# A conformer and dilated attention block on one core: attention issued in its written order, fillers split half a weight at a time, conv norm with eight diagonals

## The chip, the cores and the metric

The kernel runs on one core of a Trainium2 chip. The metric is the time of one execution on the device in microseconds: 1806.95 us, the median of three runs (1806.19 to 1810.14). The core's engines have a queue of instructions each: TensorE (PE, with its weight loads shown apart as PEld), VectorE (DVE), ScalarE (ACT), GpSimd (POOL) and SyncE (SP, which issues nearly all transfers here). An engine issues its queue in order, and a wait at the head of a queue holds all that is behind it.

## What is computed

One block over 1024 tokens of width 1024, in float32:

```
h = rms_norm(x); z = h @ w_in              # glu halves, q, k, v, two gates
a = a_val * sigmoid(a_gate)
a = silu(rms_norm(causal_depthwise_conv(a, 31 taps))); y_a = a @ w_conv_out
q, k = rms_norm per head (16 heads of 64)
o = mix of three dilated window attentions with alibi slopes; y_b = o @ w_attn_out
x = x + (sigmoid(g_a) * y_a + sigmoid(g_b) * y_b) @ w_out
h = rms_norm(x); u = depthwise_conv(h @ w_up, 3 taps)
x = x + (silu(u_gate) * u_val) @ w_down
```

The three windows share one softmax: the mask tensor of a head holds the slope's term and the logarithm of how many windows contain a pair, so the kernel takes one softmax over all causal keys.

## The kernel before, in words

Products are float32 in three passes of float32r: each operand is split into a high part (ScalarE, L76) and a low part (VectorE, L77), and high by high, high by low and low by high are summed in PSUM (`gemm_half`, L103 to L111, yields after each group of three products; such a group is called a step here). `stage` loads 512 KB of a weight into one of four `raw` buffers, `wsplit` splits it whole into one of four `whi` and `wlo` pairs.

Stages in order: the first norm and its transposes; the glu products; q, k and v, beside which VectorE computes the 31-tap convolution of eight channel blocks (`conv_branch`, `cacc`); the conv norm; attention; the output product of attention with the merge of the gates (`yb`, from L596 on); the output product, the second norm, and the feed-forward part.

Two products have nothing to wait for but their inputs and are used as fillers: the sixteen gate blocks (`gate_steps`) and, once the conv branch has been written to `da`, its output product `ya` (`side_work`). They make 384 steps. Of these, `COVER` gives three portions ahead of attention (24, 16 and 52), and `FILL` with `credit` doles out the rest in attention; what is left runs at the end of it.

The conv norm (L434 to L454): column sums of squares as products into `pss`, a reciprocal root on GpSimd (`crs`), which is spread over columns by eight products of `ones` with a diagonal tile `dg` (two buffers), copied to `sqacc`; then eight scalings by VectorE, eight SiLUs by ScalarE and eight stores to `da`.

Attention works in steps of half a head (four query blocks of 128). `step(cur, prev)` interleaves the scores of the current half with the flips and weightings of the half before. `score` (L502): two products per 512 keys into `s` (two buffers of two PSUM banks), the row minimum of negated, masked scores on VectorE (L513), the exponential with its sum on ScalarE (L515), the reciprocal on VectorE (L516), the scaling of the row on GpSimd (L517). `flip` (L520): up to four transposes of 128 x 128 into a PSUM bank `pp`, then the split into `ph` (ScalarE) and `pl` (VectorE). `weigh` (L531): two products with v into the bank `o`, up to two flips later. At the step's end ScalarE copies half of `o` to `ot` (L575) and VectorE adds it to the other half (L576). The banks `pp`, `o`, `gate` and `ya` share four buffers.

The order of instructions on each engine comes from a scheduler that runs a timing model over the program at build time and prefers what is written earlier among what it holds ready. Inside `tc.manual_schedule(engines=...)` the named engines take the order in which the instructions are written. Before the change, this holds in the first norm and at one place behind attention (L781), not in attention. A tile waits for the release of the buffer that it takes; a pool opened with `reuse_waits="tile"` waits for the tiles that lay there before.

Of the kernel before, what the change touches and what calls it, by code (L numbers as in the profile page):

```python
# [12 lines left out]
F32 = mybir.dt.float32  # L13
# [7 lines left out]
P = 128  # L21
# [13 lines left out]
FILL = (5.5, 9.5)  # L35
COVER = (24, 16, 52)
# [14 lines left out]
def block_kernel(ctx: ExitStack, tc: tile.TileContext, x, g1, g2, pack, mask,  # L51
# [95 lines left out]
    def gate_steps(hT):  # L147
        def gate(c, w, half):
            gp = bank_ps(f"gate_{c}_{half}")
            yield from gemm_half(gp, w, hT, half)  # L150
            sg = cst.tile([P, 512], F32, tag="f2", bufs=2, name=f"gs_{c}_{half}")
            act.activation(sg, gp, AF.Identity, bias=pk[:, C_GB + c : C_GB + c + 1])
            sp.dma_start(dgate[c][:, half * 512 : half * 512 + 512], sg)

        for c in range(12):
            w = wpiece(w_ch[16 + c], f"gt{c}")
            for half in range(2):
                yield from gate(c, w, half)
        ws = [wpiece(w_ch[16 + c], f"gt{c}") for c in range(12, 16)]
        for half in range(2):  # L160
            for c in range(12, 16):
                yield from gate(c, ws[c - 12], half)
            if half == 0:
                yield "half"
# [20 lines left out]
    with tc.tile_pool(name="ph1", bufs=1) as p1:  # L185
        t4 = lambda name, dt=F32: p1.tile([P, 1024], dt, tag="t4", bufs=4, name=name)
        g1r = p1.tile([1, D], F32, tag="csq", bufs=1, name="g1r")
# [168 lines left out]
        def conv_branch():  # L356
            accs = []
            for c in range(8):
# [13 lines left out]
                else:  # L372
                    sq = p1.tile([P, T], F32, tag="csq", bufs=1, name=f"csq_{c}")
# [5 lines left out]
        def qkv_head(ch, tt, ps):  # L379
# [7 lines left out]
            sq = p1.tile([P, 512], F32, tag="sq", bufs=2, name=f"sq_{ch}_{tt}")  # L387
# [5 lines left out]
            qn = p1.tile([P, 512], F32, tag="qn", bufs=3, name=f"qn_{ch}_{tt}")  # L393
# [4 lines left out]
        def qkv_tail(ch, tt, qn):  # L398
# [4 lines left out]
            qh = p1.tile([P, 512], F32R, tag="qh", bufs=2, name=f"qh_{ch}_{tt}")  # L403
            ql = p1.tile([P, 512], F32R, tag="ql", bufs=2, name=f"ql_{ch}_{tt}")
# [23 lines left out]
        gates = gate_steps(hT)  # L428
        for _ in range(COVER[0]):
            next(gates)  # L430
# [9 lines left out]
        for _ in range(COVER[1]):  # L440
            next(gates)
# [13 lines left out]
        for _ in range(COVER[2]):  # L455
            next(gates)


    with tc.tile_pool(name="ph2", bufs=1, reuse_waits="tile") as p2:
        def side_work():  # L460

            left = []
            for t in gates:
                if t == "half":
                    aT = hb_tiles(hb1, "aT")
                    left = list(range(0, KT, 2))
                    wait = 0
                elif left:
                    if wait == 0:
                        load_split(aT, da, 0, "a", [left.pop(0)])  # L470
                    wait = (wait + 1) % 7
                yield
            assert not left
            left = list(range(0, KT, 2))
            for c0 in (0, 4):
                ws = [wpiece(w_co[c], f"co{c}") for c in range(c0, c0 + 4)]
                for half in range(2):
                    for c in range(c0, c0 + 4):
                        if left:
                            load_split(aT, da, 1, "a", [left.pop(0)])  # L480
                        yp = bank_ps(f"ya_{c}_{half}")
                        yield from gemm_half(yp, ws[c - c0], aT, half)
# [64 lines left out]
        def step(cur, prev):  # L547
# [45 lines left out]
        for _ in filler:  # L593
            pass
# [537 lines left out]
```

## Time and profile before

| what | value |
|---|---|
| median of three runs | 1806.95 us |
| the profiled execution | 1806.91 us |
| its span | 1805.1 us |
| mean granted TensorE clock | 0.994 |
| TensorE busy | 1768.3 us, 98% |
| VectorE, ScalarE busy | 1314.1 us, 769.8 us |
| first product of a gate | 470.2 us |
| first score of attention | 540.0 us |
| last weighting of attention | 940.9 us |
| first product of `yb` | 969.2 us |

The times in the lower half are starts in the profiled execution. A product of 512 columns is shown as 0.389 us long, but products overlap: where TensorE is dense, it issues some 222 in 50 us, one in 0.225 us. How dense a stretch is can be told from the number of products as well as from the busy time. The granted clock (PEclk) shows where TensorE runs at half speed for a while though it is busy.

### The profile page before, as it was taken

The numbers are of one execution on the slowest core, as the hardware profiler recorded it, in microseconds if no ns is written. First come the engines' busy times: TensorE is split into PE (matmuls) and PEld (weight loads), VectorE is DVE, ScalarE is ACT, GpSimd is POOL, SyncE is SP. The second block draws the span as 40 slices with busy tenths as digits, with TensorE's granted clock in tenths as the row PEclk, the third lists the DMA queues.
The fourth block names the chain that finished last, engine by engine and source line by source line (L and its number), as shares of the span: only waits on it lengthen the run. The fifth ranks groups of instructions, "written<-read, shape, count | busy, mean of one in ns | idle before, by whom it ended". The sixth has DMA issues, their size and how long they took to land.

```text
span 1805.1 us, 22538 instructions
## 1 busy us (share of the span) xinstructions
PE 1768.3 (98%) x8248; PEld 1461.6 (81%) x8248; DVE 1314.1 (73%) x1805; ACT 769.8 (43%) x1203; POOL 182.5 (10%) x193
## 2 busy tenths in 40 slices
PE   8999999999999999999999999899999999999999
PEld 6888888888888888878888877778888888878887
DVE  7999999999635666665654563587777677679863
ACT  5111132223246666665654342455454454543431
POOL 1000142132003222122210000000000000000000
PEclk9999999999999999999999999999999999999999
DMA  5111145345468536674527566532222222399851
GB/s 215 47 47 47 43 133 175 105 135 169 136 222 231 153 122 184 196 206 148 149 76 260 178 231 213 192 105 86 89 71 93 82 80 84 117 328 327 288 175 47
DMA packets 145809, 270.16 MB, mean 150 GB/s; under 512 B 11681, under 2 KB 60961, under 8 KB 145698
## 3 DMA queue, kind: packets, MB, share of 16 engines
q1 hardware_dynamic: 145696, 268.72, 46.2%
q8 instruction: 65, 1.06, 0.3%
q14 instruction: 46, 0.38, 0.1%
q10 hardware_dynamic: 2, 0.00, 0.0%
HBM read 196.32 MB, written 72.35 MB: 149 GB/s over the span
## 4 chain that ended last, share of the span: by engine, by line
PE 50%; DMA 6%; DVE 4%; issue 2%; ACT 1%; SPq 1%; DVEq 0%; ACTq 0%
PE xz L725 5%; PE xz L724 5%; PE xz L726 5%; PE dx L977 5%; PE dy L977 4%; PE pp L524 2%; PE y L725 2%; PE y L724 2%; PE y L726 2%; DMA gg<-dya 2%; PE ya L108 2%; PE ya L109 2%; PE ya L110 2%; PE o L532 2%; PE o L533 1%
## 5 line engine op out<-in xcount | busy, mean ns | idle before, releaser
L367 DVE SCALAR_TENSOR_TENSOR cacc<-apad,pk,cacc 128x1024 f32<-128x1024 f32 x240 | 298.0, 1276 | 0.7
L125 PE MATMUL qkv<-hi_qkv,hT 128*128 128x512 f32 x384 | 151.9, 397 | 0.0
L127 PE MATMUL qkv<-hi_qkv,hT 128*128 128x512 f32 x384 | 150.5, 392 | 0.0
L126 PE MATMUL qkv<-lo_qkv,hT 128*128 128x512 f32 x384 | 149.5, 390 | 0.0
L513 DVE CUSTOM_DVE_ANT_0 p<-s,m 128x128 f32<-128x128 f32 (+7 forms) x128 | 95.1, 750 | 63.8 <-PE pp L524 42.8
L77 DVE TENSOR_TENSOR pl<-pp,ph 128x512 fp32r<-128x512 f32 x192 | 102.9, 550 | 48.7 <-ACT ph L76 48.2
L76 ACT ACTIVATE ph<-pp 128x512 fp32r<-128x512 f32 x192 | 91.1, 487 | 95.9 <-PE pp L524 93.2
L517 POOL TENSOR_SCALAR p<-p,st 128x128 f32<-128x128 f32 (+7 forms) x128 | 94.8, 749 | 335.4 <-DVE st L516 275.2
L887 DVE SCALAR_TENSOR_TENSOR u<-u,pk 128x1023 f32<-128x1023 f32 x88 | 112.3, 1277 | 2.7 <-ACT u L885 2.4
L101 POOL TENSOR_TENSOR rs<-ss,mhalf 128x8 f32<-128x8 f32 x32 | 73.8, 2311 | 338.0 <-DVE ss L100 338.0
L515 ACT ACTIVATE p<-p,st 128x128 f32<-128x128 f32 (+7 forms) x128 | 99.0, 776 | 16.3 <-DVE st L513 14.6
L108 PE MATMUL gate<-hT,hi_gt 128*128 128x512 f32 x256 | 102.1, 399 | 0.0
L109 PE MATMUL gate<-hT,hi_gt 128*128 128x512 f32 x256 | 100.8, 394 | 0.0
L110 PE MATMUL gate<-hT,lo_gt 128*128 128x512 f32 x256 | 100.3, 393 | 0.0
L524 PE MATMUL pp<-ident,p 128*128 128x128 f32 x576 | 94.1, 276 | 0.0
L127 PEld LDWEIGHTS qkv<-hi_qkv,hT 128*128 128x128 f32 x384 | 72.1, 188 | 15.4
L126 PEld LDWEIGHTS qkv<-lo_qkv,hT 128*128 128x128 f32 x384 | 72.2, 188 | 14.4
L125 PEld LDWEIGHTS qkv<-hi_qkv,hT 128*128 128x128 f32 x384 | 72.2, 188 | 14.0
L77 DVE TENSOR_TENSOR lo_uv<-raw_uv,hi_uv 128x1024 fp32r<-128x1024 f32 x21 | 25.7, 1225 | 77.8 <-ACT hi_uv L76 77.8
L524 PEld LDWEIGHTS pp<-ident,p 128*128 128x128 f32 x576 | 69.1, 142 | 9.9
L532 PE MATMUL o<-ph,v 128*128 128x512 f32 x192 | 72.7, 379 | 3.8 <-ACT ph L76 1.6
L508 PE MATMUL s<-kh,q 128*128 128x512 f32 (+1 forms) x192 | 69.3, 365 | 7.2 <-DVE st L513 7.0
(307 smaller groups left out, 4636.3 us busy)
## 6 DMA issues: line engine op xcount, KB each, us to landing
wr<-w_down SPq DMA_DIRECT2D x45, 512.0 KB, 5.5
gr<-dff SPq DMA_DIRECT2D x62, 256.0 KB, 5.1
raw_qkv<-w_qkv SPq DMA_DIRECT2D x24, 512.0 KB, 3.7
dff<-u SPq DMA_DIRECT2D x22, 512.0 KB, 2.6
raw_uv<-w_up SPq DMA_DIRECT2D x21, 512.0 KB, 3.3
raw_ug<-w_up SPq DMA_DIRECT2D x20, 512.0 KB, 3.3
dv<-v SPq DMA_DIRECT2D x16, 512.0 KB, 3.2
raw_gt<-w_ch SPq DMA_DIRECT2D x16, 512.0 KB, 4.7
```

The lines of the kernel that those rows point to most:

```text
L77: dve.tensor_tensor(out=lo, in0=src, in1=hi.bitcast(F32), op=ALU.subtract)
L108: pe.matmul(o, hi[:, k, :], ah[:, k, :], start=(k == 0), stop=False)
L109: pe.matmul(o, hi[:, k, :], al[:, k, :], start=False, stop=False)
L110: pe.matmul(o, lo[:, k, :], ah[:, k, :], start=False, stop=(k == KT - 1))
L125: pe.matmul(ps, ah, hi[:, k % 2, :], start=(k == 0), stop=False)
L126: pe.matmul(ps, ah, lo[:, k % 2, :], start=False, stop=False)
L127: pe.matmul(ps, al, hi[:, k % 2, :], start=False, stop=(k == KT - 1))
L367: dve.scalar_tensor_tensor(out=acc, in0=a[:, j : j + T], scalar=w(j), in1=acc, op0=ALU.mult, op1=ALU.add)
L524: pe.transpose(pp[:, qb * P : (qb + 1) * P], pts[qb][:, kt * P : (kt + 1) * P], ident)
L724: pe.matmul(o, wh[:, k, :], bh[:, k, :], start=(start and k == 0), stop=False, skip_group_check=not start)
L725: pe.matmul(o, wh[:, k, :], bl[:, k, :], start=False, stop=False, skip_group_check=not start)
L977: pe.matmul(banks[n], a[:, c], b[:, d], start=(start and i == 0 and m == 0), stop=(stop and i == nf - 1 and m == 2), skip_group_check=True)
```

## The change

Five things.

1. Attention (all steps and the rest of the fillers) stands in a `manual_schedule` for ScalarE, VectorE and TensorE, so that these issue it as written. Before it, the transfers of the first head are given a higher priority.
2. Each step has four slots. A slot writes: the scores of one block with minimum and exponential; fillers; the flips of this slot (one in a step whose flips are of half 0, two where they are of half 1), each followed by fillers and, from the third flip on, a weighting. Reciprocal and scaling (`share`) are written behind the slot's first flip; in the very first step they follow the next score.
3. The fillers are one generator, `side_steps`, with a list of all uses. Weights are asked for up to three uses ahead; their split is cut into halves of 512 columns that wait in a queue (`pieces`). One such half is split at the end of each slot if it is at least two slots old, and after each filler step of the covers; what a use needs and is not yet split is split on the spot. The blocks of the conv branch (`aT`) go through the same queue.
4. `COVER` is (24, 8, 20) and `FILL` (9.5, 10.5): 52 filler steps ahead of attention instead of 92, about 324 within it instead of 244, and 8 written after it.
5. In the conv norm `dg` has eight buffers. The tiles `t4`, `csq`, `sq`, `qn`, `qh` and `ql` go to a pool of their own, opened first, so that other tiles lie where attention's first tiles will be put.

```diff
-FILL = (5.5, 9.5)
-COVER = (24, 16, 52)
+FILL = (9.5, 10.5)
+COVER = (24, 8, 20)
...
+    def ask_piece(hi, lo, src):
+        pieces.append((hi, lo, src, count[2]))
+        count[0] += 1
+
+    def one_piece(age=0):
+        if pieces and count[2] - pieces[0][3] >= age:
+            hi, lo, src, _ = pieces.popleft()
+            split(hi, lo, src)
+            count[1] += 1
+
+    def side_steps(hT, da):
...
+        for i, (_, n, go) in enumerate(uses):
+            while len(got) < min(len(keys), keys.index(n) + 3):
+                k = len(got)
+                if k >= 4 and last[keys[k - 4]] >= i:
+                    break
+                w = ask_weights(src[keys[k]], keys[k])
+                got[keys[k]] = w, count[0]
+            w, need = got[n]
+            if n.startswith("co"):
+                need = max(need, marks[(i - 32) // 4 % 2])
+            while count[1] < need:
+                one_piece()
+            yield from go(w)
...
-            dg = p1.tile([P, P], F32, tag="dg", bufs=2, name=f"dg_{tt}")
+            dg = p1.tile([P, P], F32, tag="dg", bufs=8, name=f"dg_{tt}")
...
             act.activation(pt, pt, AF.Exp, bias=st[:, 0:1], scale=-1.0, accum_out=st[:, 1:2])
+            return pt, st
+
+        def share(pt, st):
             dve.reciprocal(st[:, 2:3], st[:, 1:2])
             pool.tensor_scalar(pt, pt, st[:, 2:3], 1.0, op0=ALU.mult, op1=ALU.mult)
-            return pt
...
             for n in range(4):
+                count[2] += 1
                 if cur is not None:
-                    pts.append(score(cur[0], cur[2], cur[1] * 4 + n))
+                    late = (pt, st) if prev is None and n else None
+                    pt, st = score(cur[0], cur[2], cur[1] * 4 + n)
+                    pts.append(pt)
+                    if late:
+                        share(*late)
                 fill(rate)
-                if prev is not None:
-                    for kt in range(n * nkt // 4, (n + 1) * nkt // 4):
-                        pend.append(flip(h, half, ppts, kt))
-                        fill(rate)
-                        if len(pend) > PEND:
-                            weigh(o, v, nkt, *pend.pop(0))
+                kts = [] if prev is None else range(n * nkt // 4, (n + 1) * nkt // 4)
+                for kt in kts:
+                    pend.append(flip(h, half, ppts, kt))
+                    if cur is not None and kt == kts[0]:
+                        share(pt, st)
+                    fill(rate)
+                    if len(pend) > PEND:
+                        weigh(o, v, nkt, *pend.pop(0))
+                if cur is not None and prev is None and n == 3:
+                    share(pt, st)
+                one_piece(2)
...
-        nxt = head(0)
+        with tc.high_priority(600):
+            nxt = head(0)
...
+        with tc.manual_schedule(engines={ENG.Activation, ENG.DVE, ENG.PE}):
```

More of the change, by code (lines that the diff above doesn't have):

```diff
@@ L145, in block_kernel @@
     dform = [[dr.tile([P, 1024], F32R, name=f"dform{f}_{i}") for i in range(7)] for f in range(2)]
[L147 to L153, printed above, removed]
+    HALVES = (slice(0, 512), slice(512, 1024))
@@ L454, in block_kernel @@
             sp.dma_start(da[:, c, :], ct)
-        for _ in range(COVER[2]):
-            next(gates)
+        cover(COVER[2])
     with tc.tile_pool(name="ph2", bufs=1, reuse_waits="tile") as p2:
[L460 to L482, printed above, removed]
-                        ya = cst.tile([P, 512], F32, tag="f2", bufs=2, name=f"ya_{c}_{half}")
-                        act.activation(ya, yp, AF.Copy)
-                        sp.dma_start(dya[c][:, half * 512 : half * 512 + 512], ya)
         def head(h):
```

107 lines of the change are left out of this document (77 added, 30 removed).

## The prediction

> **What bounds the kernel now.** First the page: busy shares and the chain.
>
> ```profile
> PE 1768.3 (98%) x8248; PEld 1461.6 (81%) x8248; DVE 1314.1 (73%) x1805; ACT 769.8 (43%) x1203; POOL 182.5 (10%) x193
> PE 50%; DMA 6%; DVE 4%; issue 2%; ACT 1%; SPq 1%; DVEq 0%; ACTq 0%
> ```
>
> TensorE is the bound. The change leaves its products as they are, so it can only move TensorE's idle and slow time. Next, the table of stretches around the change, and two short ones inside it.
>
> ```profile
> core 0: us, PE busy (x) PEld busy (x) DVE busy (x) ACT busy (x) POOL busy (x), PEclk, DMA share, GB/s
> 470.00:540.00 70.00, 69.68 (x322) 57.91 (x321) 28.65 (x33) 24.48 (x30) 1.64 (x1) 1.00 0.59 192
> 540.00:760.00 220.00, 213.18 (x1145) 179.49 (x1144) 133.42 (x356) 137.51 (x299) 55.41 (x76) 0.98 0.63 178
> 760.00:945.00 185.00, 178.42 (x960) 148.93 (x959) 112.81 (x276) 114.37 (x241) 39.41 (x52) 0.99 0.50 146
> 945.00:969.00 24.00, 24.00 (x107) 19.88 (x106) 14.14 (x14) 15.81 (x20) 0.00 (x0) 1.00 1.01 363
> 646.00:649.80 3.80, 1.82 (x13) 1.39 (x12) 3.80 (x6) 2.64 (x7) 0.50 (x1) 1.00 0.70 171
> 649.80:653.40 3.60, 3.60 (x14) 3.29 (x15) 3.09 (x11) 2.97 (x7) 2.10 (x2) 0.53 1.06 264
> ```
>
> Conv norm (470 to 540) is dense. Attention with its fillers (540 to 945) idles 13.4 us, and three spells of 3.4 us at half clock (544, 650, 810) cost some 5 us more. From 945 to 969 only fillers run. Who makes TensorE wait:
>
> ```profile
> PE s L508 <- DVE st L513: 7.0, 10, 1.3
> PE o L533 <- DVE pl L77: 1.8, 1, 1.8
> PE o L532 <- ACT ph L76: 1.6, 2, 1.1
> ```
>
> So VectorE and ScalarE are late now and then. The view that decides is VectorE's own order in one step with long rows:
>
> ```profile
> 717.66 1.08 DVE L513 CUSTOM_DVE_ANT_0 p<-s,m 128x896 f32<-128x896 f32 x1
> ...
> 718.66 0.16 DVE L516 RECIPROCAL st<-st 128x1 f32<-128x1 f32 x1
> 718.74 0.41 DVE L77 TENSOR_TENSOR pl<-pp,ph 128x256 fp32r<-128x256 f32 x1
> 719.06 1.22 DVE L513 CUSTOM_DVE_ANT_0 p<-s,m 128x1024 f32<-128x1024 f32 x1
> ...
> 720.20 0.29 DVE L77 TENSOR_TENSOR pl<-pp,ph 128x128 fp32r<-128x128 f32 x1
> 720.40 0.16 DVE L516 RECIPROCAL st<-st 128x1 f32<-128x1 f32 x1
> 721.60 0.16 DVE L516 RECIPROCAL st<-st 128x1 f32<-128x1 f32 x1 [1.04 <-ACT p L515]
> ```
>
> The next row minimum (719.06) is issued ahead of the reciprocal (720.40) of the row before, so VectorE works while ScalarE takes the exponential. Minima stand 1.4 us apart. The prices, by shape:
>
> ```profile
> L513 DVE CUSTOM_DVE_ANT_0 p<-s,m 128x1024 f32<-128x1024 f32 x16 | 19.4, 1214 | 0.0
> L515 ACT ACTIVATE p<-p,st 128x1024 f32<-128x1024 f32 x16 | 18.5, 1155 | 1.8 <-DVE st L513 1.8
> L515 ACT ACTIVATION_READ_ACCUMULATOR p<-p,st 128x1 f32 x128 | 24.4, 190 | 0.0
> L77 DVE TENSOR_TENSOR pl<-pp,ph 128x128 fp32r<-128x128 f32 x32 | 9.0, 282 | 8.6 <-ACT ph L76 8.5
> L76 ACT ACTIVATE ph<-pp 128x128 fp32r<-128x128 f32 x32 | 8.9, 277 | 19.7 <-PE pp L524 19.4
> L516 DVE RECIPROCAL st<-st 128x1 f32<-128x1 f32 x128 | 19.8, 157 | 15.7 <-ACT p L515 14.9
> ```
>
> **Conv norm and covers.** With eight diagonals the eight small products need no longer alternate with VectorE (499 to 511 now). They stood between dense fillers, so this saves TensorE 0.5 us (three gaps of 0.16 us among them). From 470.2: 24 filler steps (0.68 us each: three products at the dense 0.2265 us), 1.8 us of column sums, 8 steps, 1.8 us for the diagonals, 20 steps: attention starts at 509.1 instead of 540. Diagonals end about 492, the eight scalings 506, the SiLUs 508, so the norm is hidden behind the 20 steps. The moved fillers are not lost work; they sit in attention. The pool is parted so that the first head's tiles no longer lie over the conv sums. I cost that at nothing; if its fetches waited as now (526.8 to 541), up to 15 us would go. The SP queue keeps its order of needs; fetches for the next head have half a head, 14 us, to land.
>
> **Attention in written order.** Per slot, VectorE now gets: minimum, `pl` of the first flip, reciprocal, `pl` of the second flip (if any), perhaps half a weight's low part, next minimum. ScalarE gets: exponential, `ph`, `ph`, perhaps half a high part. `ph` stands behind the exponential, `pl` needs `ph`, the reciprocal stands behind `pl`, and the next minimum behind the reciprocal. That is one serial loop.
>
> Step B (scores of half 1, flips of half 0), widths 640, 768, 896, 1024: minimum 822, 950, 1082, 1214 ns; exponential 829, 937, 1045, 1155; accumulator read 190; `ph` 595, 483, 377, 277; `pl` 686, 546, 413, 282; reciprocal 157. Each slot sums to 3.27 us. The timeline shows instructions of one engine overlapping by 0.08 to 0.1 us (four times) and 0.04 us for each of two hops: 3.0 a slot, 12.0 a step. Before it the last step's output must leave: last product to copy 0.3, L575 0.593, L576 0.683 and a hop, 1.6 us, because the first minimum now queues behind L576. So 13.6. Fillers add to the loop: 52 half splits over 33 steps, 1.6 a step by 0.6 us of VectorE (0.68 at 512 wide, less overlap), and a gate's copy (0.678) that falls between exponential and `ph` in about half the steps: 1.3 together. B takes 14.9 us.
> TensorE's own work in B: scores 2.95, ten transposes at 0.109, weighting 1.13, 10.5 filler steps 7.14, some 0.3 for waits: 12.6. So it waits 2.3 us, at the last weighting.
>
> Step A (scores of half 0, flips of half 1): the loop is 11.0 + 1.6 + up to 1.3 = 13.9. TensorE: 1.13 + 2.83 + 2.94 + 9.5 steps 6.46 + 0.3 = 13.7, plus a wait at its first flip for the last row of B: reciprocal, hop, 1.125 on POOL (the row at 1024), hop, 1.4 after the last `pl`, against 0.7 of TensorE's work: 0.7. A takes 14.4.
>
> Sum: 509.1 + first step 4.9 + 16 x 14.9 + 15 x 14.4 + last step without scores 12.5 + the 8 steps left over 5.4 = 986.3. Before, the next stage's first product (`yb`) starts at 969.2: **+17**.
>
> **Half clock.** The spell at 650 followed gaps of 1.3 and 0.7 us, that at 810 gaps of 1.1 and 1.8, that at 544 gaps of 0.6, 0.9 and 0.9; lone gaps of 0.8 (622, 793) or 1.4 (1594) brought none. After each B some 3.0 us idle stand within 4. A spell costs 1.7 us, and A has no room for it. From none to all 16 steps: 0 to 27 us; I take half, **+13.6**, as the gaps vary with the half splits. The Trainium skill ("TensorE: Matmul & The Clock Gate", Part 1) states that the slow clock comes after at least one idle window of about 3.4 us; no gap here is that long, so by it this term would be 0 and the sum 1827, but the spells at 650 and 810 came after shorter gaps.
>
> **Hand-over.** The first `ao` weight is split only at 963.7 to 964.9, 23.7 us after attention's last product (940.9): staging buffers pass through eight loads of `do` first. Filler hid that. After the change 5.4 us of filler remain. The high and low parts of half 0 can run beside the last step, where ScalarE and VectorE are slack; if nothing moves, 18 us of idle. I take 3, nearer to the slack, and keep 0 and 18.
>
> Sum against the profiled execution's 1806.9 (span 1805.1 and 1.8 around it; the median of the runs is the same): 1806.9 + 17 + 13.6 + 3 = **1840**.
>
> **Rivals.**
> Fed TensorE (faster): the loop is shorter than TensorE's work. It decides below 12.6 us for B. Then B 12.6, A 13.7, first step 2: 936, 33 us gained, less the hand-over: 1775 to 1796. For it: filler per head rises from 16 steps to 20, and the same busy times overlap well today. Against it: the order above, unless the engines are not given the written order.
> Loop without additions: half splits and copies fall into waits, no spell. B 13.6, A 14.4, attention ends 21 us sooner than in my sum: 1803, and 1796 to 1811 with the small costs.
> No spells, else as mine: 1827, as the skill's rule would have it. For it: single gaps stay under 2.4 us.
> Spells at every head and an uncovered hand-over: 1806.9 + 17 + 27 + 18 = 1869.
>
> **Numbers.** Loop-bound 0.49 (1815 to 1860, spells few or many: 0.17 for none, 0.32 with them), worst case 0.10, without additions 0.16 (split faster 0.07, same 0.06, slower 0.03), fed 0.25. Faster 0.32, same 0.06, slower 0.62. A measurement of this kernel tells 0.2%, 3.6 us, from no change. Leaving one in ten out on each side: 1785 to 1868; the likeliest alone 1818 to 1860.
>
> **What would show it.** In VectorE's timeline the reciprocal of a row stands ahead of the next minimum, minima 3 us or more apart in B. TensorE's waits are led by `o` L533 on `pl` and by transposes on POOL's `p`, near 45 us in all, and half-clock spells follow B. `yb` starts near 1000. Attention's first score is near 509. I am wrong if minima stay closer than TensorE's slots, if the waits of attention fall under 13 us, or if a stall at `yb` or at the first fetch exceeds 10.

## The result and the profile after

The changed kernel takes 1879.63 us (median of four runs, 1876.83 to 1880.86), against 1807.38 us for the kernel before, run beside it: 1.0397 times as long, with a 95% interval of 1.0381 to 1.0412. The forecast was 1840 us with a range of 1785 to 1868. The direction was right; the time lies 12 us above the range. The profiled execution took 1880.86 us with a span of 1879.0, 73.9 us more than before, where the sum had +33.6.

The engines' busy times and the chain that ended last, on the page of the changed kernel:

```profile
PE 1787.4 (95%) x8248; PEld 1456.3 (78%) x8248; DVE 1321.8 (70%) x1837; ACT 774.9 (41%) x1235; POOL 194.8 (10%) x193
...
PE 75%; DVE 7%; issue 6%; DMA 6%; ACT 5%; SPq 1%; POOL 0%; DVEq 0%; ACTq 0%
```

TensorE has the same 8248 products and is no longer busy for 98% of the span but for 95%; the chain runs through VectorE for 7% of the span where it was 4%. The table of stretches shows where (columns as before: length, busy time and instructions of each engine, granted clock, DMA share, GB/s):

```profile
core 0: us, PE busy (x) PEld busy (x) DVE busy (x) ACT busy (x) POOL busy (x), PEclk, DMA share, GB/s
470.00:510.00 40.00, 39.66 (x191) 33.05 (x189) 25.37 (x36) 20.41 (x25) 1.64 (x1) 1.00 0.61 217
510.00:540.00 30.00, 19.10 (x82) 15.44 (x82) 8.07 (x26) 8.36 (x20) 4.88 (x7) 0.77 0.87 230
540.00:760.00 220.00, 202.15 (x1022) 160.25 (x1023) 110.45 (x289) 113.76 (x251) 47.06 (x57) 0.98 0.49 136
760.00:945.00 185.00, 167.14 (x845) 130.92 (x844) 100.55 (x252) 100.20 (x221) 38.33 (x47) 0.99 0.52 151
1021.00:1045.00 24.00, 5.80 (x25) 4.49 (x24) 12.69 (x13) 15.69 (x20) 0.00 (x0) 0.70 0.90 308
```

Three places lose time: the first head (510 to 540, 11 us idle and a low clock), the steps (from 540 on, 8 to 10% idle where it was 3 to 4%), and the hand-over (1021 to 1045, 18 us idle). The covers (470 to 510) are dense, as forecast. Behind them nothing has changed: from the first product of `yb` (1044.4, before 969.5; the 969.2 of the table before is the start of its weight load) to the end it is 834.6 us, before 835.7. The waits of the attention stage (us in total, times, longest; `X <- Y` is X waiting for Y):

```profile
ACT p L561 <- DVE st L559: 200.4, 128, 12.4
DVE pl L78 <- ACT ph L77: 190.5, 143, 2.2
...
PE yb L109 <- ACT hi_ao L77: 18.2, 1, 18.2
PE o L580 <- ACT ph L77: 13.2, 16, 1.5
PE pp L572 <- ACT gs L192: 12.3, 15, 1.1
PE s L554 <- DMA kh<-dk: 10.0, 1, 10.0
...
PE pp L572 <- POOL p L566: 0.8, 4, 0.2
...
PE o L580 <- DVE pl L78: 0.8, 2, 0.6
```

In the kernel before, the same two waits stand at the end of these lines (busy time, mean ns, idle time before and what ended it):

```profile
L77 DVE TENSOR_TENSOR pl<-pp,ph 128x512 fp32r<-128x512 f32 x192 | 102.9, 550 | 48.7 <-ACT ph L76 48.2
L515 ACT ACTIVATE p<-p,st 128x128 f32<-128x128 f32 (+7 forms) x128 | 99.0, 776 | 16.3 <-DVE st L513 14.6
```

VectorE and ScalarE now wait for each other in nearly every slot, 190 and 200 us in all, where it was 48 and 15. The reason is in VectorE's timeline of a step B (start, length, idle time before and its releaser):

```profile
712.25 0.83 DVE L559 CUSTOM_DVE_ANT_0 p<-s,m 128x640 f32<-128x640 f32 x1
...
715.27 0.69 DVE L78 TENSOR_TENSOR pl<-pp,ph 128x512 fp32r<-128x512 f32 x1 [2.19 <-ACT ph L77]
715.88 0.15 DVE L565 RECIPROCAL st<-st 128x1 f32<-128x1 f32 x1
715.95 0.94 DVE L559 CUSTOM_DVE_ANT_0 p<-s,m 128x768 f32<-128x768 f32 x1
...
718.91 1.07 DVE L559 CUSTOM_DVE_ANT_0 p<-s,m 128x896 f32<-128x896 f32 x1
```

This is the loop that the prediction described: the reciprocal stands ahead of the next minimum, and the minima shown are 3.7 and 3.0 us apart (the pair of long rows that the prediction shows for the kernel before: 1.4).

Sizes, from one `ot` to the next: a step A (scores of half 0, flips of half 1) takes 15.9 us on the mean, a step B 15.2; forecast were 14.4 and 14.9 ahead of half-clock spells.

### The profile page after: what moved, and what is told of

It is laid out like the page before. It is cut to its first block, busy times and chain, and to the rows that moved or that the text cites. A ratio compares the mean times of both kernels' runs of the same rounds, so it can differ in the third digit from the quotient of the medians.

```text
span 1879.0 us, 22641 instructions
## 1 busy us (share of the span) xinstructions
PE 1787.4 (95%) x8248; PEld 1456.3 (78%) x8248; DVE 1321.8 (70%) x1837; ACT 774.9 (41%) x1235; POOL 194.8 (10%) x193
## 4 chain that ended last, share of the span: by engine, by line
PE 75%; DVE 7%; issue 6%; DMA 6%; ACT 5%; SPq 1%; POOL 0%; DVEq 0%; ACTq 0%
PE dx L1038 6%; PE xz L785 5%; PE xz L786 5%; PE xz L787 5%; PE dy L1038 5%; PE qkv L126 5%; PE qkv L128 5%; PE qkv L127 5%; DVE p L559 3%; DMA gg<-dya 2%; PE pp L572 2%; PE y L785 2%; PE y L787 2%; PE y L786 2%; PE gate L109 2%
## 5 line engine op out<-in xcount | busy, mean ns | idle before, releaser
L78 DVE TENSOR_TENSOR pl<-pp,ph 128x512 fp32r<-128x512 f32 x192 | 106.2, 555 | 190.8 <-ACT ph L77 190.5
L566 POOL TENSOR_SCALAR p<-p,st 128x128 f32<-128x128 f32 (+7 forms) x128 | 105.5, 825 | 412.5 <-DVE st L565 292.0
L572 PE MATMUL pp<-ident,p 128*128 128x128 f32 x576 | 98.3, 278 | 19.9 <-ACT gs L192 12.3
L572 PEld LDWEIGHTS pp<-ident,p 128*128 128x128 f32 x576 | 73.6, 142 | 55.3 <-ACT gs L192 18.7
L109 PE MATMUL gate<-hT,hi_gt 128*128 128x512 f32 x256 | 110.8, 433 | 2.8 <-DVE pl L78 2.4
L559 DVE CUSTOM_DVE_ANT_0 p<-s,m 128x128 f32<-128x128 f32 (+7 forms) x128 | 95.5, 746 | 19.2 <-DMA m<-mask 15.7
L110 PE MATMUL gate<-hT,hi_gt 128*128 128x512 f32 x256 | 102.0, 398 | 0.0
L77 ACT ACTIVATE ph<-pp 128x512 fp32r<-128x512 f32 x192 | 90.3, 481 | 16.5 <-PE pp L572 13.9
L580 PE MATMUL o<-ph,v 128*128 128x512 f32 x192 | 71.4, 372 | 14.0 <-ACT ph L77 13.2
L126 PEld LDWEIGHTS qkv<-hi_qkv,hT 128*128 128x128 f32 x384 | 72.1, 188 | 13.9
L554 PE MATMUL s<-kh,q 128*128 128x512 f32 (+1 forms) x192 | 68.9, 359 | 10.2 <-DMA kh<-dk 10.0
```

The costliest lines, as they stand in the source:

```text
L78: dve.tensor_tensor(out=lo, in0=src, in1=hi.bitcast(F32), op=ALU.subtract)
L109: pe.matmul(o, hi[:, k, :], ah[:, k, :], start=(k == 0), stop=False)
L126: pe.matmul(ps, ah, hi[:, k % 2, :], start=(k == 0), stop=False)
L559: dve.tensor_tensor_reduce(out=pt, in0=s[:, :nk], in1=m[:, u0 : u0 + nk], scale=-1.0, scalar=3e38, op0=ALU.add, op1=ALU.min, accum_out=st[ ...
L572: pe.transpose(pp[:, qb * P : (qb + 1) * P], pts[qb][:, kt * P : (kt + 1) * P], ident)
```

## The experiments

Each ratio is to the kernel before in runs beside it, with its 95% interval. "Steps" are means of 15 intervals between `ot` copies. The scheduler is called the planner in the expectations.

### Is it the order? Four runs

**e1_order** writes the exponential behind the slot's flips, and the reciprocal behind the next minimum.

```diff
-            act.activation(pt, pt, AF.Exp, ...)      # in score()
+        def grow(pt, st):
+            act.activation(pt, pt, AF.Exp, ...)
...
+                    due = (pt, st) if n else None
                     pt, st = score(cur[0], cur[2], cur[1] * 4 + n)
...
+                    if due:
+                        share(*due)
...
                     pend.append(flip(h, half, ppts, kt))
-                    if cur is not None and kt == kts[0]:
-                        share(pt, st)
...
+                if cur is not None:
+                    grow(pt, st)
+                    if n == 3:
+                        share(pt, st)
```

> The changed kernel with one thing moved: in every slot the exponential is written behind the slot's flips, and the reciprocal and GpSimd's scaling of a row behind the next row's minimum (for the fourth row at the end of its slot). Nothing is added or left out. Theory (the written order closes the loop minimum, exponential, high copy, low part, reciprocal, next minimum): the loop opens, VectorE's waits for ph fall from 190 us to under 60, steps B fall from 15.2 us to about 13 and steps A from 15.7 to about 14, so 1835 us (1820 to 1845). Rival (the lost time is PSUM waits behind the gate's and ya's copies, the hand-over and the first fetch, whatever the order): within 8 us of the changed kernel's 1880.

Measured: 1818.24 us, ratio 1.0067 (1.0052 to 1.0082). That is 61 us less than the changed kernel, and 2 us below the expected range. Steps A fell to 14.2 us, B to 12.8, and VectorE's order reads:

```profile
716.16 0.80 DVE L559 CUSTOM_DVE_ANT_0 p<-s,m 128x640 f32<-128x640 f32 x1
...
717.48 0.69 DVE L78 TENSOR_TENSOR pl<-pp,ph 128x512 fp32r<-128x512 f32 x1 [0.51 <-ACT ph L77]
718.30 0.96 DVE L559 CUSTOM_DVE_ANT_0 p<-s,m 128x768 f32<-128x768 f32 x1
```

The low part shown now waits 0.5 us instead of 2.2, and this pair of minima is 2.1 us apart. All waits of low parts fell from 190.5 to 65.9 us, a little above the 60 expected, and of TensorE's long waits only the two single stalls are left:

```profile
DVE pl L78 <- ACT ph L77: 65.9, 120, 1.0
...
PE yb L109 <- ACT hi_ao L77: 16.8, 1, 16.8
...
PE s L554 <- DMA kh<-dk: 10.1, 1, 10.1
```

So the same instructions, fillers and half splits in another written order lose 61 us less. The waits of flips behind gate copies (12.3 us above) vanish too, so they came with the loop.

**e2_scheduler** takes the written order away and keeps everything else.

```diff
-        with tc.manual_schedule(engines={ENG.Activation, ENG.DVE, ENG.PE}):
+        if True:
```

> The changed kernel without the written order: attention's instructions are ordered by the planner again, everything else of the change stays (the late fillers, the eight diagonals, the half splits, the reciprocal inside the slot). Theory (the written order is the cost, the rest of the change is neutral within 15 us): 1810 us (1795 to 1825). Rival (moving filler steps into attention, half splits and the later hand-over are the cost, order or not): 1850 us or more.

Measured: 1829.76 us, ratio 1.0132 (1.0115 to 1.0149). It lies between the two expectations: by the ratios 48 us of the 72 are the order's, and 24 remain, more than the theory allowed. In its trace TensorE stands 20.3 us ahead of `yb` and 4.9 ahead of the first score.

**e11_planner_portions** asks what these 24 us are (23 in the expectation): the same, with the covers and rates of the kernel before.

```diff
-FILL = (9.5, 10.5)
-COVER = (24, 8, 20)
+FILL = (5.5, 9.5)
+COVER = (24, 16, 52)
```

> The changed kernel without the written order and with the portions of the kernel before (covers of 24, 16 and 52; 5.5 and 9.5 in a half head). What is left of the change: half splits, the reciprocal's place in the code, one list of fillers, eight diagonals, the parted pool. Theory (the 23 us by which the kernel without the written order was slower than before are the uncovered hand-over and first fetch, and nothing else of the change costs): 1806 us (1800 to 1812). Rival (half splits and the written place of the reciprocal cost by themselves): 1818 or more.

Measured: 1806.78 us, ratio 0.9996 (0.9982 to 1.0011). No long stall is left ahead of the first score or of `yb`. So, under the scheduler's order, half splits, the place of the reciprocal in the code, the single list of fillers, the eight diagonals and the parted pool cost nothing together; the 24 us came with the portions, that is with fewer fillers around attention.

**e3_before_written** puts the written order on the kernel before and changes nothing else.

```diff
+        with tc.manual_schedule(engines={ENG.Activation, ENG.DVE, ENG.PE}):
             for h in range(H):
...
```

> The kernel before with one thing added: VectorE, ScalarE and TensorE take attention's instructions in the order in which its code states them; fillers, split sizes and conv norm stay as before. Theory (the written order alone makes the serial loop): slots of B near 3 us and steps near 15 us instead of a mean of 12.1, so 1860 us (1840 to 1890). Rival (the order is harmless and the rest of the change costs): 1807 us, within 10.

Measured: 1913.58 us, ratio 1.0594 (1.0568 to 1.0620), 24 us above the expected range. The order alone is dearer there than with the rest of the change. Two waits stand out: the reciprocal is written right behind the exponential (VectorE waits 119.8 us for it, a line that the changed kernel has at 0.8), and whole weights are split on the spot (`gate` waits 30.8 us for `hi_gt`). They suggest that the late reciprocal and the half splits soften what the order does; no run separates the two.

### Which instruction closes the loop? Two runs

**e6_share** moves only the reciprocal and the scaling behind the next minimum.

```diff
+                    due = (pt, st) if n else None
                     pt, st = score(cur[0], cur[2], cur[1] * 4 + n)
...
+                    if due:
+                        share(*due)
...
-                    if cur is not None and kt == kts[0]:
-                        share(pt, st)
...
+                if cur is not None and n == 3:
+                    share(pt, st)
```

> The changed kernel with only the reciprocal and GpSimd's scaling moved behind the next row's minimum; the exponential stays ahead of the flips' copies. Theory (the loop closes over exponential, ph and pl, the reciprocal lies in it with 0.16 us a row at most, and GpSimd's rows come later): 1875 us (1865 to 1885). Rival (the reciprocal's wait on the exponential is what holds VectorE, so that moving it frees the loop like moving the exponential did): 1818 to 1835 us.

Measured: 1877.50 us, ratio 1.0403 (1.0374 to 1.0431); steps 15.7 and 15.1. The reciprocal was in the loop but not what made it.

**e15_exp_only** moves only the exponential; the reciprocal follows at once.

```diff
-            act.activation(pt, pt, AF.Exp, ...)      # in score()
+        def grow(pt, st):
+            act.activation(pt, pt, AF.Exp, ...)
...
-                    if cur is not None and kt == kts[0]:
-                        share(pt, st)
...
+                if cur is not None:
+                    grow(pt, st)
+                    share(pt, st)
```

> The changed kernel with only the exponential moved behind the slot's flips; the reciprocal follows it at once, ahead of the next row's minimum. Theory (the loop's long part is exponential, ph, pl; without ph and pl in it, minimum, exponential, reciprocal take about 2.4 us a slot in B, under TensorE's 12.6 us a step even with the output copy): within 12 us of the kernel that has both moves, 1818 to 1830 us. Rival (VectorE waits for the exponential at each reciprocal, and a loop over it costs as much as the one over the flips): 1850 us or more.

Measured: 1832.47 us, ratio 1.0149 (1.0134 to 1.0164), 2.5 us past the range; steps 14.4 and 13.5. The exponential's place is worth 45 of the 60 us. With it moved, the reciprocal's place is worth the other 15, though it was worth nothing alone: VectorE's wait for the exponential at a reciprocal is longer here than in e1_order (the lines of the two runs, in this order):

```profile
DVE st L567 <- ACT p L564: 45.0, 67, 1.1
...
DVE st L567 <- ACT p L564: 23.7, 32, 1.1
```

### How long is the loop itself? Two runs

**e10_bare** gives the steps no fillers at all.

```diff
-FILL = (9.5, 10.5)
+FILL = (0, 0)
```

> The changed kernel with no fillers inside the steps (0 and 0 instead of 9.5 and 10.5); all that is left runs behind attention. This measures the loop by itself. My sums without copies and splits of fillers: steps B 13.6 us, steps A 11.0. If these hold, the fillers' copies and splits are what makes the steps 15.2 and 15.7, and the time is near 1980 us (1965 to 1995). Rival (the loop of step A was summed too short, its second flip of a slot lies in the loop as well): steps A of 13 us or more, 2010 us.

Measured: one run of 2056.22 us; attention's last weighting at 948.9, then 272 us of fillers that TensorE does not run densely (their weights are split on the spot). The total is therefore no measure of the loop; the steps are. B took 13.9 us, A 12.9. The expectation gave 11.0 for A and left out the output copy of 1.6 that the prediction's sum has, 12.6; by its own words the 12.9 was all but the rival's 13. What the rival says is true as well: the second flip's low part stands ahead of the next minimum. But the prediction's 11.0 already holds it (the four minima, exponentials, reads, reciprocals and first flips come to 10.2, the second low parts to 2.2, and the overlaps take 1.4 off). So the bare sums of the prediction, 13.6 and 12.6, hold within 0.3 us. Four slots of a step B, VectorE's timeline:

```profile
659.92 0.81 DVE L559 CUSTOM_DVE_ANT_0 p<-s,m 128x640 f32<-128x640 f32 x1
...
663.02 0.94 DVE L559 CUSTOM_DVE_ANT_0 p<-s,m 128x768 f32<-128x768 f32 x1
...
665.99 1.07 DVE L559 CUSTOM_DVE_ANT_0 p<-s,m 128x896 f32<-128x896 f32 x1
...
668.95 1.21 DVE L559 CUSTOM_DVE_ANT_0 p<-s,m 128x1024 f32<-128x1024 f32 x1
```

Spacings of 3.10, 2.97 and 2.96 us stand against 3.0 in the prediction. Loop and TensorE's work are then known apart: A 12.9 bare and 14.2 when TensorE sets it (e1_order), B 13.9 and 12.8. In the changed kernel A takes 15.9, more than either. B takes 15.2, which is the bare loop and the 1.3 that the prediction added for half splits and copies.

**e5_early** tests a cause for that excess, the flips that wait for PSUM banks behind the gates' copies: it writes the copy right behind the bank's last product (`but_last` hands on all steps but the last), for `ya` too.

```diff
-                yield from gemm_half(gp, w, hT, half)
+                yield from but_last(gemm_half(gp, w, hT, half))
                 ...
                 sp.dma_start(dgate[c][:, half * 512 : half * 512 + 512], sg)
+                yield
```

> The changed kernel with ScalarE's copy of a finished gate or ya bank written right behind the bank's last product instead of at the next filler step; the order of attention stays. Theory A (steps A are longer than I summed because flips wait for PSUM banks behind these copies, 18.6 us in the changed kernel): these waits go below 5 us, steps A fall from 15.7 to about 14.6, the time to 1863 us (1857 to 1868). Theory B (the loop of VectorE and ScalarE sets the step, and a copy costs ScalarE the same 0.68 us of the loop wherever it stands in a slot): within 6 us of 1880, with TensorE's idle time moved to the weightings.

Measured: 1874.52 us, ratio 1.0386 (1.0357 to 1.0415). Those waits went, and the waits of weightings on `ph` rose from 13.2 to 20.7 us; A only fell from 15.9 to 15.7. Theory B holds, and that cause of the excess falls. The trace of the changed kernel shows two things of it. The step A from 978.8, the one with a single copy beside it and no half-clock spell, takes 14.7 us; the eight steps A with five copies and half splits take 15.8 to 16.0, where e1_order has 14.2 to 14.7 for the same steps. And waits go both ways: TensorE for the two engines in the lines above, these two for its transposes (`ph` on `pp`, 13.9 us). A reading that fits, not shown by a run of its own, is that long slots make TensorE wait and short ones make the other two wait, and that neither gets its time back.

### Fillers: are they free in the loop?

**e4_cover** moves 16 filler steps ahead of attention.

```diff
-FILL = (9.5, 10.5)
-COVER = (24, 8, 20)
+FILL = (9.0, 10.0)
+COVER = (24, 8, 36)
```

> The changed kernel with 16 of the filler steps moved back ahead of attention (36 instead of 20 in the last cover, 9 and 10 per half head instead of 9.5 and 10.5). Theory (the loop sets the length of a step and fillers beside it are nearly free, so only the cover of the first fetch is gained, and 16 x 0.68 = 10.9 us of filler time is paid ahead): first score near 529 with no idle time ahead of it, steps shorter by about 0.3 us each from fewer copies, 1880 us (1868 to 1886). Rival (TensorE's own work sets the steps, so that fillers taken out of them shorten them by their full 0.34 us, and the 13 us of idle time at the first fetch goes): 1866 us (1860 to 1870).

Measured: 1886.19 us, ratio 1.0442 (1.0420 to 1.0464), slower than the changed kernel. The first stall fell from 10.0 to 2.6 us, nearly as both said. The steps did not shorten (16.1 and 15.0), so 10.9 us of fillers were paid ahead for nothing.

**e9_portions** does the like with the loop open (e1_order), and leaves more steps behind attention (29 by the trace), outside the written order.

```diff
-FILL = (9.5, 10.5)
-COVER = (24, 8, 20)
+FILL = (8.25, 9.25)
+COVER = (24, 8, 36)
...
-            for _ in filler:
-                pass
+        for _ in filler:
+            pass
```

> The kernel with the exponential behind the flips and the reciprocal behind the next minimum (1818 us), with the fillers' portions set back to near those of the kernel before: 36 instead of 20 in the last cover, 8.25 and 9.25 instead of 9.5 and 10.5 in a half head, some 33 steps left over behind attention and outside the written order. Theory (with the loop open TensorE's own work sets the steps, so fillers can be moved freely, and 10 us of idle time at the first fetch and 17 us ahead of yb are covered by them): steps shorter by the 0.85 us that each gives up, no idle stretch over 3 us at either place, 1791 us (1785 to 1798), faster than the kernel before. Rival (the steps stay at 14.15 and 12.8 us, as in the changed kernel, where fillers were moved without gain): 1825 to 1840.

Measured: 1810.80 us, ratio 1.0017 (1.0005 to 1.0029). Now the steps did shorten, to 13.8 and 12.3, and the two stalls are 3.2 and 3.1 us. But it gained 9 us on e1_order, not 27: `yb` starts only 10 us sooner. Between the first `ot` and the last there are 35 filler steps fewer, 24 us of work, and the time there fell by 12.5 us; 6.7 of the missing 11 came back as idle time. With less filler in them the steps are no longer TensorE's alone: the loop comes near again.

### First fetch and hand-over, one by one

These four start from e1_order, where TensorE sets the steps.

**e7_first** issues the `da` stores from ScalarE.

```diff
-            sp.dma_start(da[:, c, :], ct)
+            act.dma_start(da[:, c, :], ct)
```

> The kernel with the exponential behind the flips and the reciprocal behind the next minimum (1818 us), and one more edit: the eight da stores are issued by ScalarE instead of SyncE, so that the first head's fetch doesn't stand behind them. Theory (the fetch is late because it stands on SyncE's queue behind stores that wait for the SiLUs): it issues near 495, attention's first score starts at 509 instead of 520 without an idle stretch or a half-clock spell there, 1806 us (1802 to 1812). Rival (the fetch waits for memory or for the transfers themselves): 1814 to 1822.

Measured: 1819.70 us, ratio 1.0084 (1.0065 to 1.0103): no gain. SyncE's timeline says why (start, time at issue):

```profile
508.05 0.32 SPq L193 DMA_DIRECT2D dgate<-gs  x1
508.46 0.99 SPq L134 DMA_DIRECT2D q<-dq  x1
```

Behind the `da` stores stood another store, of the cover's last gate, whose copy on ScalarE ended at 508.0. Taking one thing away from the head of a queue showed the next.

**e12_fetch_queue** leaves SyncE's queue altogether: head 0 is fetched by GpSimd.

```diff
+            get = fetch_by(pool if h == 0 else sp)
             for s in range(2):
-                fetch(q[s * DH : (s + 1) * DH, :], ...)
+                get(q[s * DH : (s + 1) * DH, :], ...)
...
```

> The kernel with the exponential behind the flips and the reciprocal behind the next minimum (1818 us), with one more edit: the eight transfers of head 0 are issued by GpSimd instead of SyncE. Theory (the fetch is late because it stands on SyncE's queue behind the stores of the conv branch and of the fillers' last gates, and only the queue holds it): it issues before 500, the first score starts at 510 instead of 520, no half-clock spell there, 1805 us (1800 to 1810). Rival (the memory under the tiles or the transfers themselves hold it): 1814 to 1822.

Measured: 1810.06 us, ratio 1.0028 (1.0018 to 1.0037). GpSimd's timeline:

```profile
488.55 1.64 POOL L102 TENSOR_TENSOR crs<-css,mhalf 128x8 f32<-128x8 f32 x1 [50.51 <-DVE css L101]
490.13 0.74 POOL L137 DMA_DIRECT2D q<-dq  x1
...
493.94 0.56 POOL L137 DMA_DIRECT2D v<-dv  x1
```

The first score starts at 509.1 and nothing stalls there. So neither memory nor the transfers held the fetch; the queue's order did. Of the 10 us at `yb`, 4 went again in the stages behind it in this execution; the ratio is 0.0039 lower, 7 us.

**e8_handover** frees the last step and the leftover fillers from the written order, and writes the `ao` weights ahead of half 1's loads.

```diff
-            step(None, prev)
-            for _ in filler:
-                pass
+        step(None, prev)
+        for _ in filler:
+            pass
...
-        for half in range(2):
-            load_split(oT, do_, half, "o")
+        load_split(oT, do_, 0, "o")
+        ws = [wpiece(w_ao[c], f"ao{c}") for c in range(4)]
```

> The same kernel (1818 us) with another edit: the last step and the fillers left over stand outside the written order, and the first four ao weights are written behind the loads of half 0 of the attention output and ahead of those of half 1. Theory (17 us of idle time before yb come from the written order's end and from the order of loads on SyncE): idle time before yb under 4 us and no half-clock spell there, 1801 us (1797 to 1806). Rival (the loads wait for the last step's result or for staging buffers in any order): 1812 to 1820.

Measured: 1816.04 us, ratio 1.0056 (1.0040 to 1.0073), not told from e1_order. The stall ahead of `yb` fell from 16.8 to 12.9 us, but the last weighting came 4.5 us later. The splits of `oT` still came behind the last output copy although ScalarE was idle for 4.8 us ahead of it, and the `ao` loads waited for staging buffers that these splits free.

**e13_ao** takes the weights away from that: three `ao` weights follow the fillers' weights through the list of half splits, so that they are loaded and split inside the last steps.

```diff
-        keys = list(dict.fromkeys(n for _, n, _ in uses))
+        keys = list(dict.fromkeys(n for _, n, _ in uses)) + ["ao0", "ao1", "ao2"]
...
+        while len(got) < len(keys):
+            k = keys[len(got)]
+            got[k] = ask_weights(src[k], k), count[0]
+        while pieces:
+            one_piece()
...
-            load_split(oT, do_, half, "o")
+        load_split(oT, do_, 0, "o")
+        ws = [got[n][0] for n in AO] + [wpiece(w_ao[3], "ao3")]
...
+                if half and not c0:
+                    load_split(oT, do_, 1, "o")
...
```

> The same kernel (1818 us) with another edit: the first three ao weights follow the fillers' weights through the same list of half splits, inside the written order, and the loads of half 1 of the attention output are written behind half 0's merges. Theory (yb is late because its weights pass the staging buffers behind eight loads of the attention output, and because no split behind the written order starts before it ends): yb starts 4 to 8 us after the last weighting instead of 22, 1804 us (1799 to 1810). Rival (yb waits for the last step's output whatever the weights do): 1814 to 1820.

Measured: 1807.33 us, ratio 1.0011 (1.0000 to 1.0021). `yb` starts 5.6 us after the last weighting instead of 22.5, with a stall of 3.8 us. The rival falls: not the last step's output but the way of the weights through the buffers held it. Of the 17 us some 6 went again behind `yb` (841.8 us from there to the end, 835.4 in e1_order); what takes them was not tried. The run also writes half 1's loads behind half 0's merges, a move that e8_handover has too.

### Together, with and without the written order

**e14_all**: e1_order, e12_fetch_queue and e13_ao, with a few more steps left over (14 by the trace, the expectation has 18).

```diff
-FILL = (9.5, 10.5)
+FILL = (9.2, 10.2)
```

> All of these together: exponential behind the flips, reciprocal behind the next minimum, head 0 fetched by GpSimd, ao weights through the list of half splits, covers as in the changed kernel, 9.2 and 10.2 steps in a half head and some 18 left over outside the written order. Theory (three separate losses that add up: the loop 61 us, the fetch 13, the hand-over 17): 1790 us (1784 to 1797), faster than the kernel before by 0.6 to 1.2%. Rival (the idle time comes back elsewhere, as steps that are longer or a later stall behind yb): 1800 or more.

Measured: 1797.48 us, ratio 0.9957 (0.9943 to 0.9971): 0.4% faster than the kernel before and 82 us faster than the changed one. The expected 1790 was 7 us too hopeful: the single losses don't add up in full. Its stretches show TensorE busy for 413.7 of the 422 us of steps, and for all 10 us behind the last weighting:

```profile
510.00:530.00 20.00, 18.21 (x94) 14.74 (x92) 8.90 (x29) 11.31 (x24) 6.00 (x8) 1.00 1.04 306
530.00:952.00 422.00, 413.74 (x2208) 344.14 (x2207) 262.44 (x635) 251.65 (x552) 91.08 (x120) 1.00 0.54 153
952.00:962.00 10.00, 10.00 (x46) 8.29 (x45) 5.48 (x7) 6.49 (x9) 0.00 (x0) 1.00 0.89 288
```

**e16_planner_all** is the same with the scheduler's order (and the reciprocal and exponential where the change has them).

```diff
-        with tc.manual_schedule(engines={ENG.Activation, ENG.DVE, ENG.PE}):
+        if True:
```

> The changed kernel without the written order, with head 0 fetched by GpSimd, the ao weights through the list of half splits, and 9.2 and 10.2 steps in a half head. Theory (the planner's order keeps attention as dense as the opened loop does, and what it lost was only fetch and hand-over): 1803 us (1796 to 1809). Rival (the opened written order is what makes the best kernel faster than the one before): 1812 or more.

Measured: 1798.81 us, ratio 0.9969 (0.9958 to 0.9980). It is not told apart from e14_all. It differs from e11_planner_portions, which was level with the kernel before, in the fetch, the `ao` weights and the portions that these allow. So that is where the gain over the kernel before comes from; a written order that keeps the loop open is as good as the scheduler's, and no better.

## Why the prediction was wrong

The steps of the sum, from left to right in time. The forecast for `yb` was 986.3 + 13.6 + 3 = 1002.9; it came at 1044.4, 41.5 us later. The stages behind were forecast unchanged and are, within 1.1 us.

- **What bounds, and the loop.** Right. Order, spacing of minima (3.0), and bare steps (13.6 and 12.6 summed, 13.9 and 12.9 run) are as worked out. e1_order and e15_exp_only show that the exponential ahead of the flips closes the loop. Wrong is where TensorE waits: named were `o` on `pl` and transposes on GpSimd's `p`, which took 0.8 us each. In the steps it waits some 40 us, near the 45 forecast, but for `ph` (13.2 in all) and for banks behind the copies `gs` and `ya` (12.3 and 6.3).
- **The rivals.** A fed TensorE (0.25) fell with the 190 us of waits: the engines were given the order as written. The loop without additions (0.16) fell too, with B at 15.2 and not 13.6. No spells (0.17) came near in its own term, 5.1 us, and missed by the others. The worst case at 1869 counted two of the late places and not the third, and so the range ended short. The prediction's own signs of being wrong included a stall over 10 us at `yb` or at the first fetch: they were 18.2, and 10.0 with 0.9 more right behind it.
- **First fetch, costed at nothing, bound 15.** Wrong: the first `ot` came 12.4 us later than summed, 10.0 of it the stall at the first score. The step that failed is that a parted pool frees the fetch. Memory was free (e12_fetch_queue issues the same fetch from 490.1 on and nothing waits for it); the fetch stood on SyncE's queue behind stores that waited for the SiLUs and for the last gate's copy. The prediction said of that queue only that it keeps its order, and did not ask what stands ahead in it. SyncE in the changed kernel:

```profile
508.78 0.53 SPq L528 DMA_DIRECT2D da<-cacc  x1
509.41 0.73 SPq L134 DMA_DIRECT2D q<-dq  x1
```

- **Steps, 14.9 and 14.4.** B took 15.2, A 15.9: 27.5 us over the stage from the first `ot` to the last (479.5, summed 452). By step, the 15 B give 4.6, the 15 A 22.2 and the last step 0.7. B is the bare loop (13.9 for 13.6) and its additions as summed. The term that was mis-sized is A. It was taken as the longer of two chains, the loop with additions (13.9) and TensorE's work (13.7), and one wait of 0.7. Apart, the loop takes 12.9 without additions and TensorE's chain 14.2 (e1_order, its waits included), as long as summed or nearly so; together they take 15.9. So the step that failed is the overlap of the two. Some 3 of the 22 us are two half-clock spells (next point). With one copy beside it A takes 14.7, with five copies and half splits 15.8 to 16.0, so most of the rest comes with these; why it isn't hidden stays open.
- **Half clock, +13.6 for eight spells in the steps.** Three came (604, 727, 850), 5.1 us, two in steps A and one in a B. These lie inside the 27.5 above. The term was too large by 8.5 and so hid a part of the other misses; the section at the end says why.
- **Hand-over, +3 with 18 as the upper end.** Wrong: 18.2 us idle. The step that failed is "the high and low parts of half 0 can run beside the last step, where ScalarE and VectorE are slack". They were slack and were not used. ScalarE in the changed kernel:

```profile
1020.77 0.60 ACT L633 ACTIVATE ot<-o 64x512 f32<-64x512 f32 x1 [1.88 <-PE o L581]
1021.39 0.60 ACT L203 ACTIVATE ya<-ya 128x512 f32<-128x512 f32 x1
1021.89 3.89 ACT L77 ACTIVATE oT<-raw_o 128x1024 fp32r<-128x1024 f32 x4
...
1043.33 1.06 ACT L77 ACTIVATE hi_ao<-raw_ao 128x1024 fp32r<-128x1024 f32 x1 [0.85 <-DMA raw_ao<-w_ao]
```

  The splits of `oT` follow the last copy of the written block, eight loads pass the four staging buffers, and the first `ao` weight is split 22.6 us after `ot`. Before the change the way was as long (23.7 in the prediction); the filler that hid it was moved.
- **Conv norm, −0.5.** The diagonals ended at 492 and the scalings at 506, as summed; a gain of that size can't be told in these runs.

Against 41.5: fetch and first step 12.4, steps 27.5 less the 13.6 of half clock, hand-over 15.2. At the fetch and the hand-over the right size stood in the text as an upper bound, and the low end was taken because something could cover it. That the direction came out right is no luck, since the loop is as described.

## What to carry to other kernels

An order written by hand is a set of loops: for each slot, follow one result around all engines back to the instruction that opens the next slot, and write what nobody waits for soon behind what others wait for (here the exponential behind the flips' copies, worth 45 of 60 us). A filler that is moved takes its cover with it: look up what it hid at its old place, and price that stall in full unless the work under it is really issued earlier, in each queue, the transfers' too. Where two chains in a step are within a few per cent of each other, take more than the longer one (here 15.9, for a TensorE chain of 14.2 and a loop summed to 13.9).

## What the runs showed of the hardware

In every one of the 18 profiled executions the half-clock stretches start on a grid of 3.4133 us (off it by at most 0.004 of a grid step) and last whole grid windows, but for one that the end of the execution cuts. Laid over TensorE's gaps between 100 and 1780 us, the grid gives, for windows at full clock:

| idle in the window, us | windows | next window at half clock |
|---|---|---|
| under 1.1 | 8397 | 0 |
| 1.1 to 1.7 | 123 | 18 |
| 1.7 to 2.0 | 15 | 13 |
| 2.0 and more | 91 | 91 |

A window already at half clock is followed by another at less idle time: all 99 with 0.9 us and more, 7 of 11 with 0.5 to 0.9, 5 of 36 with less, none of 87 with under 0.01. Four times 2.1 to 2.5 us of idle time fell within 3.4 us across the border of two windows, and no half clock followed (e4_cover at 602, for one). So by these traces not a single gap counts, nor gaps within some 4 us, as the prediction took it, but the idle sum of one fixed window; between 1.1 and 2.0 us that sum does not decide alone. A head of the changed kernel has some 2.6 us idle, near the 3.0 forecast, but most of it in pieces of 0.3 to 1.6 us (43 of them in the steps), which mostly fall into different windows; in three cases 1.2 to 1.7 us fell into one. The Trainium skill ("TensorE: Matmul & The Clock Gate", Part 1) gives a free-running window of 3413 ns, with which the grid agrees; that the window must be idle as such does not agree, since 2.0 us of idle time in it were always enough here (91 of 91). By its rule the term would be 0, by the prediction's 13.6; 5.1 us were measured.

A stretch that TensorE waits through in pieces also shows more busy time for the same products: from 545 us to the last weighting the changed kernel has 435.7 us for 2210 products, e1_order 408.7 for 2200. Some 5 us are half clock and 2 the ten products; the rest fits that a product which stands alone is shown with its 0.389 us and one in a dense row takes 0.227. Idle time alone (39.8 against 4.4 us in the steps) understates such a loss.
